# A hybrid decoder block on one core: the convolution's copies go to another queue, and one gate pair leaves the seven-product form

## The chip, the cores and the metric

The kernel runs on one core of one Trainium2 chip. The metric is device microseconds of one execution. Three runs of the kernel before gave 1552.89, 1555.58 and 1556.43 us; the median is 1555.58. One more execution was taken by the profiler, and every duration below is from it.

Five engines work in parallel, each through its own queue in order: TensorE (PE; its weight loads are listed as PEld), VectorE (DVE), ScalarE (ACT), GpSimd (POOL) and SyncE (SP, which here only starts DMAs). An instruction that waits holds up all that stands behind it on its engine. DMAs can be started from SP, ACT and POOL.

## What is computed

One decoder block over 256 tokens of width 2048, in fp32:

```python
proj = h_norm @ w_in          # q, k, v, g_out, gk_low, gate_b, gate_c, xc, merge_a, merge_b
o    = rmsnorm(gla_chunked(q, k, v, log_g), gla_norm_w)      # 4 heads, value width 512
y_a  = o * silu(g_out)
y_b  = gate_b * causal_depthwise_conv(gate_c * xc, conv_w)   # 3 taps: rows t, t-1, t-2
merged = sigmoid(merge_a) * y_a + sigmoid(merge_b) * y_b
h    = x + merged @ w_out
out  = rmsnorm(h + swiglu(rmsnorm(h, ffn_norm_w)), final_norm_w)
```

The change is in the stage that computes the six gate projections (g_out, gate_b, gate_c, xc, merge_a, merge_b, each 2048 columns), the convolution, and `merged`.

## The kernel before

**Pieces.** Every weight matrix is read in pieces of 128 x 1024 fp32 (512 KB), two blocks of 128 input rows by 512 columns. Each fp32 number is split into two rounded parts: ACT casts `hi` from `raw` (L217), DVE computes `lo = raw - hi` (L222). A product is then three matmuls (`mm3`, L326 to L328): lo with the high part of the activations, hi with their low part, hi with high. There are 5 `raw`, 6 `hi` and 5 `lo` buffers; `take` keeps 5 pieces loaded ahead of the one that PE uses. Each used piece is one tick of a counter.

**Eights.** A key such as `g0` (the first 512 columns of g_out; the digit is the group of 512 columns, 0 to 3) is 8 pieces of 12 matmuls, 6 for each half of the tokens. Its two sums lie in the PSUM banks `b5` and `ax1`, the same two for every key. After the last piece a function `done` reads them out. So a key's first 6 matmuls wait until `b5` has been read out, the next 6 until `ax1` has.

**Sevens.** A pair of keys (`gc0` with `xc0`, say) can be computed with seven block products in place of eight, `sevens` (L374), in four quarters: per quarter the plain block "11", the sums "t1", "t3", "t2", "t4", and later "21" and "22". That is 28 pieces of 6 matmuls, 168, where two keys as eights take 16 pieces of 12, 192. The price is on the other engines: 28 casts and 28 subtractions in place of 16, and one DVE sum for each of the 16 t-pieces (L238, L244), made in place in a tile `x` that ACT and DVE must first have read.

**The gate stage.** `GATES` (L73) lists six steps. A step names one pair for sevens and the keys for eights; `mixed` (L105) spreads the pieces of the eights over the gaps between the 28 pieces, first behind the t-pieces. In the kernel before the steps are: g0 alone; gc0+xc0 with ma0, gb0; gc1+xc1 with mb0, g1, ma1; gc2+xc2 with gb1, mb1, g2, ma2; gc3+xc3 with gb2, mb2; gb3+mb3 with g3, ma3. So five of twelve pairs are sevens.

What happens behind a key, for group i: `g` makes `ya` = silu(g) * o; `ma` multiplies `ya` by sigmoid(ma); `gb` is copied to `sb`; `mb` multiplies `sb` by sigmoid(mb) and then calls `merge`. The two sigmoids are done in `gated` (L843): ACT writes the sigmoid of one token half into a tile `scr` (L847), of which there is one buffer, and DVE multiplies (L848). The pair gc+xc gives `u` = gate_c * xc (L882).

**The convolution.** Two ticks later `conv_shift` (L805) has ACT start six DMAs (L814 to L819) that copy `u` into `u1` and `u2`, one and two tokens later; the taps come by one more (L811). Eight ticks later `conv_sum` (L821) has DVE make five operations on 128 x 1024, three products (L827 is u2's, L828 u1's, L829 u's) and two sums (L830, L831). `merge` (L833) multiplies `sb` by that, adds `ya` (L835, L836), and puts the four 128 x 128 transposes of each token half (L544) into PE's order, then ACT's and DVE's split of them (L546, L547) into `mh`, `ml`, which the output projection `wo` reads.

The ticks of `later` and `at` give the order in which the program issues the work. A scheduler behind it then orders each engine's queue by what it reckons to be ready, so the queues don't follow the ticks strictly. The sums of input blocks that sevens need are made from x at ticks 34, 40, 46, 52 (`x_blocks`, L710), in the attention stage, ahead of the gate stage.

After the gate stage, `wo` runs (4 keys as eights, other banks); the pool `ew` of the gate stage is closed behind wo0, and POOL loads x again into its place (L926) for the residual sum (L928). Then the feed-forward part, with five more pairs as sevens.

Of the kernel before, what the change touches and what calls it, by code (L numbers as in the profile page):

```python
# [43 lines left out]
def plan():  # L44
# [27 lines left out]

GATES = (  # L73
    (None, ("g0",)),
    (("gc0", "xc0"), ("ma0", "gb0")),
    (("gc1", "xc1"), ("mb0", "g1", "ma1")),
    (("gc2", "xc2"), ("gb1", "mb1", "g2", "ma2")),
    (("gc3", "xc3"), ("gb2", "mb2")),
    (("gb3", "mb3"), ("g3", "ma3")),
)  # L80

HIDDEN = (
# [16 lines left out]
def seven_list(pair):  # L99

    out = [(what, q) for q in range(4) for what in ("11", "t1", "t3", "t2", "t4")]
    return [(pair, e) for e in out + [(what, q) for q in range(4) for what in ("21", "22")]]


def mixed(step, early=False):  # L105

    pair, keys = step
    eights = [(key, k) for key in keys for k in range(0, KC, 2)]
    if pair is None:
        return eights  # L110
    sevens = seven_list(pair)
    sums = ("t1", "t3", "t2", "t4")
    gaps = [0] * len(sevens)
    rest = len(eights)
    while rest > 0:
        for some in (sums + ("11",) if early else sums, ("21", "22")):
            for n, (_, e) in enumerate(sevens):
                if e[0] in some and rest > 0:
                    gaps[n] += 1
                    rest -= 1  # L120
    out, put = [], 0
    for e, n in zip(sevens, gaps):
        out += [e] + eights[put:put + n]
        put += n
    return out


def gates_list():
    return [e for i, step in enumerate(GATES) for e in mixed(step, i == 4)]


def hidden_list(part):
# [33 lines left out]
def block_kernel(ctx, tc, x, xt, cols_in, gkw_in, gku_in, gnw, conv_w, finw, w_in, w_out, w_gu, w_dn, out):  # L166
# [7 lines left out]
    junk_pool = ctx.enter_context(tc.tile_pool(name="junk", bufs=1))  # L174
# [117 lines left out]
    def later(delay, fn):  # L292

        pending.append((count["tick"] + delay, fn))
# [15 lines left out]
    def one_at_a_time(delay, fn):  # L310

        spaced.append((count["tick"] + delay, fn))
# [189 lines left out]
                                op=ALU.subtract)  # L502

    xv = x.rearrange("(t p) d -> p t d", p=P)


    xs0 = wraw.tile([P, 4, T], F32, tag="raw", name="xs")
# [5 lines left out]


    def square_sum(src, acc):
        junk = junk_pool.tile([P, 512], mybir.dt.bfloat16, tag="junk", name="junk")
        nc.scalar.activation(junk[:, :src.shape[-1]], src, AF.Square, accum_out=acc)

    def rstd_of(ss, n, r):
# [20 lines left out]
    def transpose_block(src, t, hi, lo):  # L540

        ps = bank([P, 4, P], "trb", "ax0")
        for j in range(4):
            nc.tensor.transpose(out=ps[:, j, :], in_=src[:, j * P:(j + 1) * P], identity=ident)  # L544
# [148 lines left out]
    def at(tick, fn):  # L693
        later(tick - count["tick"], fn)
# [15 lines left out]
    def x_blocks(q):  # L710
        pair = gpool.tile([P, NM, T], F32, tag="bc", name="xraw")
        raw, work = pair[:, 0:4, :], pair[:, 4:8, :].rearrange("p s (j c) -> p s j c", c=P)
        cs = slice(4 * q, 4 * q + 4)
        nc.vector.tensor_tensor(out=raw, in0=xh[:, cs, :].bitcast(F32), in1=xl[:, cs, :].bitcast(F32), op=ALU.add)
        sum_blocks(raw, q, xsums, work)

    for q in range(4):
        at(34 + 6 * q, lambda q=q: x_blocks(q))


    def decayed(i, kr, qr):
# [78 lines left out]
    oside = None  # L800
    mix = ExitStack()
    mh, ml = [None] * 4, [None] * 4
    us, ya, sb = {}, {}, {}

    def conv_shift(i):  # L805
# [3 lines left out]
        us[i] = (us[i], u1, u2, taps)  # L809
        u = us[i][0]  # L810
        nc.scalar.dma_start(taps, conv_w[:, :, i * 512:(i + 1) * 512].to_broadcast([P, 3, 512]))  # L811
        nc.gpsimd.memset(u1[0:1, 0, :], 0.0)
        nc.gpsimd.memset(u2[0:2, 0, :], 0.0)
        nc.scalar.dma_start(u1[1:113, :, :], u[0:112, :, :])  # L814
        nc.scalar.dma_start(u1[113:128, :, :], u[112:127, :, :])
        nc.scalar.dma_start(u1[0:1, 1, :], u[127:128, 0, :])
        nc.scalar.dma_start(u2[2:114, :, :], u[0:112, :, :])
        nc.scalar.dma_start(u2[114:128, :, :], u[112:126, :, :])
        nc.scalar.dma_start(u2[0:2, 1, :], u[126:128, 0, :])  # L819

    def conv_sum(i):  # L821
        u, u1, u2, taps = us[i]

        def taps_of(j):
            return taps[:, j:j + 1, :].to_broadcast([P, NT, 512])

        nc.vector.tensor_tensor(out=u2, in0=u2, in1=taps_of(0), op=ALU.mult)  # L827
        nc.vector.tensor_tensor(out=u1, in0=u1, in1=taps_of(1), op=ALU.mult)  # L828
        nc.vector.tensor_tensor(out=u, in0=u, in1=taps_of(2), op=ALU.mult)  # L829
        nc.vector.tensor_tensor(out=u1, in0=u1, in1=u2, op=ALU.add)  # L830
        nc.vector.tensor_tensor(out=u, in0=u, in1=u1, op=ALU.add)  # L831

    def merge(i, ts):  # L833

        nc.vector.tensor_tensor(out=sb[i][:, ts, :], in0=sb[i][:, ts, :], in1=us[i][0][:, ts, :], op=ALU.mult)  # L835
        nc.vector.tensor_tensor(out=sb[i][:, ts, :], in0=sb[i][:, ts, :], in1=ya[i][:, ts, :], op=ALU.add)  # L836
        if mh[i] is None:
            mh[i] = omain.tile([P, 4, T], F32R, tag=f"m{i}", name="mh")
            ml[i] = oside.tile([P, 4, T], F32R, tag=f"m{i}", name="ml")
        for t in range(ts.start, ts.stop):  # L840
            one_at_a_time(2, lambda t=t: transpose_block(sb[i][:, t, :], t, mh[i], ml[i]))

    def gated(dst, ps):  # L843

        for t in range(NT):
            scr = ew.tile([P, 512], F32, tag="scr", name="scr")
            nc.scalar.activation(scr, ps[t], AF.Sigmoid, scale=r1[:, t:t + 1])  # L847
            nc.vector.tensor_tensor(out=dst[:, t, :], in0=dst[:, t, :], in1=scr, op=ALU.mult)  # L848

    def gate(key):  # L850
        i = int(key[-1])

        def done(ps):
            if key[:-1] == "g":
                ya[i] = ew.tile([P, NT, 512], F32, tag="ya", name="ya")
                for t in range(NT):
                    nc.scalar.activation(ya[i][:, t, :], ps[t], AF.Silu, scale=r1[:, t:t + 1])
                nc.vector.tensor_tensor(out=ya[i], in0=ya[i], in1=o[i], op=ALU.mult)
            elif key[:-1] == "gb":
                sb[i] = ew.tile([P, NT, 512], F32, tag="sb", name="sb")  # L860
                for t in range(NT):
                    nc.scalar.activation(sb[i][:, t, :], ps[t], AF.Copy, scale=r1[:, t:t + 1])
            elif key[:-1] == "ma":
                gated(ya[i], ps)
            else:
                gated(sb[i], ps)
                merge(i, slice(0, NT))

        return done

    def gate_pair(pair):
        i = int(pair[0][-1])

        def second(t):
            to = us if pair[0][:-1] == "gc" else sb
            if i not in to:
                to[i] = ew.tile([P, NT, 512], F32, tag="u" if to is us else "sb", name="u" if to is us else "sb")
            return to[i][:, t, :]

        def done(t, one, two):  # L880
            if pair[0][:-1] == "gc":
                nc.vector.scalar_tensor_tensor(out=two, in0=one, scalar=r1sq[:, t:t + 1], in1=two,  # L882
                                               op0=ALU.mult, op1=ALU.mult)
                if t == 0:
                    later(2, lambda: conv_shift(i))
                    later(8, lambda: conv_sum(i))
            else:
                nc.scalar.activation(two, two, AF.Sigmoid, scale=r1[:, t:t + 1])
                nc.vector.scalar_tensor_tensor(out=two, in0=one, scalar=r1[:, t:t + 1], in1=two,
                                               op0=ALU.mult, op1=ALU.mult)  # L890

                later(3 if t else 1, lambda: merge(i, slice(t, t + 1)))

        return second, done
# [22 lines left out]
    h = dpool = None  # L917
# [138 lines left out]
    assert not pending and not spaced and not ready and count["loaded"] == len(stream) + 1  # L1056


H_AT = (2, 4, 6, 8)
SQ_AT = (5, 7, 9, 11)  # L1060
WARM = 9
# [54 lines left out]
```

## Time and profile before

| what | us |
|---|---|
| median of 3 runs | 1555.58 |
| the profiled execution | 1552.18 |
| its span, first to last instruction | 1550.3 |
| PE busy in it | 1508.5 |
| DVE busy | 1205.4 |
| ACT busy | 839.4 |
| POOL busy | 20.8 |
| gate stage, first to last matmul of a gate | 212.5 to 744.8 |
| step 1 (gc0) begins | 236.3 |
| step 2 (gc1) | 319.1 |
| step 3 (gc2) | 431.0 |
| step 4 (gc3) | 560.6 |
| step 5 (gb3 with mb3) | 653.1 |

Times are from the start of the span. A row of the timeline gives start, duration, engine, line, operation, out<-in and, in brackets, the idle time of the engine just before and what ended it. A row of the waits reads "who waited for whom: us in total, times, longest". A row by windows gives, for a stretch, its length and the busy time and number of instructions of each engine, then the granted clock, the share of DMA time and GB/s. An engine name with a q is its sequencer, which issues DMAs and waits.

### The profile page before, as it was taken

To read this page: it belongs to the slowest core of one execution; us is meant where nothing else is said; L and a number is where in the kernel's file an instruction comes from. 1 tells how busy PE (TensorE), PEld (TensorE's weight loads), DVE (VectorE), ACT (ScalarE), POOL (GpSimd) and SP (SyncE) were. 2 spreads that over 40 slices of the span, in tenths; PEclk is the share of its full clock that TensorE was granted. 3 is DMA by queue.
4 is the path that set the end of the run, shared out by engine and by line. 5 is a ranking of instruction groups with operands and counts; after the bars stand their busy time and mean duration, and the time that the engine had idled before them with its cause. 6 is when DMAs were issued, how large, how long until landed. Compare 5 with 4: busy or idle time off the path is not lost.

```text
span 1550.3 us, 19386 instructions
## 1 busy us (share of the span) xinstructions
PE 1508.5 (97%) x7129; PEld 1256.5 (81%) x7129; DVE 1205.4 (78%) x1208; ACT 839.4 (54%) x947; POOL 20.8 (1%) x33
## 2 busy tenths in 40 slices
PE   9989999989999999889999999999999999999997
PEld 8979988868878787668788888788888888888887
DVE  5887548989879778989768998955889975678664
ACT  6755446645645545456556565633555553455543
POOL 0020000000000000000000000000000000000000
PEclk9999999999999999999999999999999999999999
DMA  9645557877876868768865777866676886676862
GB/s 318 219 149 164 174 162 251 275 237 240 277 229 215 296 176 269 233 209 284 308 181 162 245 229 254 301 206 188 203 262 206 272 281 192 182 222 200 249 222 90
DMA packets 98182, 350.18 MB, mean 226 GB/s; under 512 B 11084, under 2 KB 11212, under 8 KB 97960
## 3 DMA queue, kind: packets, MB, share of 16 engines
q1 hardware_dynamic: 94080, 337.97, 67.3%
q10 hardware_dynamic: 3432, 8.89, 2.3%
q0 software_dynamic: 576, 2.10, 0.4%
q8 instruction: 56, 0.92, 0.2%
q14 instruction: 38, 0.31, 0.1%
HBM read 342.64 MB, written 2.10 MB: 222 GB/s over the span
## 4 chain that ended last, share of the span: by engine, by line
PE 85%; DVE 5%; DMA 4%; issue 2%; ACT 2%; POOL 1%; ACTq 0%; SPq 0%; DVEq 0%
PE fg L326 7%; PE fg L328 7%; PE fg L327 7%; PE dn L326 5%; PE dn L328 5%; PE dn L327 5%; DVE lo L222 3%; PE fu L326 3%; PE fu L327 3%; PE fu L328 3%; PE gc L326 2%; PE gc L328 2%; PE gc L327 2%; DMA raw<-in_w_in_dram 2%; PE ma L326 2%
## 5 line engine op out<-in xcount | busy, mean ns | idle before, releaser
L222 DVE TENSOR_TENSOR lo<-raw,hi 128x1024 fp32r<-128x1024 f32 (+1 forms) x513 | 621.6, 1218 | 194.2 <-PE dn L326 76.3
L217 ACT CAST hi<-raw 128x1024 fp32r<-128x1024 f32 (+1 forms) x513 | 532.8, 1049 | 372.9 <-PE dn L328 116.0
L217 ACT CAST hi<-x 128x1024 fp32r<-128x1024 f32 x120 | 126.3, 1053 | 230.6 <-DVE x L244 153.4
L222 DVE TENSOR_TENSOR lo<-x,hi 128x1024 fp32r<-128x1024 f32 x120 | 146.8, 1223 | 45.4 <-ACT hi L217 32.3
L326 PE MATMUL dn<-lo,acth 128*128 128x512 f32 (+1 forms) x376 | 141.6, 377 | 0.3 <-ACT sg L965 0.3
L327 PE MATMUL dn<-hi,actl 128*128 128x512 f32 (+1 forms) x376 | 141.2, 376 | 0.0
L328 PE MATMUL dn<-hi,acth 128*128 128x512 f32 (+1 forms) x376 | 141.1, 376 | 0.0
L326 PE MATMUL fg<-lo,hh 128*128 128x512 f32 x312 | 122.6, 393 | 0.0
L327 PE MATMUL fg<-hi,hl 128*128 128x512 f32 x312 | 121.6, 390 | 0.0
L328 PE MATMUL fg<-hi,hh 128*128 128x512 f32 x312 | 121.5, 390 | 0.0
L244 DVE TENSOR_TENSOR x<-x,raw 128x1024 f32<-128x1024 f32 x80 | 97.6, 1220 | 4.9 <-DMA raw<-in_w_in_dram 2.6
L326 PEld LDWEIGHTS dn<-lo,acth 128*128 128x128 f32 x376 | 70.8, 188 | 13.4 <-ACT sg L965 0.7
L328 PEld LDWEIGHTS dn<-hi,acth 128*128 128x128 f32 x376 | 70.8, 188 | 12.8
L327 PEld LDWEIGHTS dn<-hi,actl 128*128 128x128 f32 x376 | 70.8, 188 | 12.6
L326 PE MATMUL fu<-lo,hh 128*128 128x512 f32 x192 | 74.7, 389 | 0.0
L328 PE MATMUL fu<-hi,hh 128*128 128x512 f32 x192 | 74.7, 389 | 0.0
L327 PE MATMUL fu<-hi,hl 128*128 128x512 f32 x192 | 74.7, 389 | 0.0
L328 PEld LDWEIGHTS fg<-hi,hh 128*128 128x128 f32 x312 | 58.6, 188 | 12.4
L326 PEld LDWEIGHTS fg<-lo,hh 128*128 128x128 f32 x312 | 58.6, 188 | 12.3 <-ACT hraw L534 0.3
L327 PEld LDWEIGHTS fg<-hi,hl 128*128 128x128 f32 x312 | 58.6, 188 | 11.7
L326 PE MATMUL fg<-lo,sh 128*128 128x512 f32 x160 | 62.9, 393 | 0.0
L328 PE MATMUL fg<-hi,sh 128*128 128x512 f32 x160 | 62.4, 390 | 0.0
(256 smaller groups left out, 3060.6 us busy)
## 6 DMA issues: line engine op xcount, KB each, us to landing
raw<-in_w_in_dram SPq DMA_DIRECT2D x255, 512.0 KB, 4.5
raw<-in_w_gu_dram SPq DMA_DIRECT2D x176, 512.0 KB, 4.5
raw<-in_w_dn_dram SPq DMA_DIRECT2D x88, 512.0 KB, 3.6
raw<-in_w_out_dram SPq DMA_DIRECT2D x32, 512.0 KB, 4.5
y<-in_w_in_dram SPq DMA_DIRECT2D x20, 512.0 KB, 5.3
x<-in_w_in_dram SPq DMA_DIRECT2D x20, 512.0 KB, 4.5
y<-in_w_gu_dram SPq DMA_DIRECT2D x20, 512.0 KB, 5.2
x<-in_w_gu_dram SPq DMA_DIRECT2D x20, 512.0 KB, 6.7
```

Source lines behind the costliest of these rows:

```text
L217: nc.scalar.copy(hi[:, ks, :], raw[:, ks, :])
L222: nc.vector.tensor_tensor(out=lo[:, ks, :], in0=raw[:, ks, :], in1=hi[:, ks, :].bitcast(F32), op=ALU.subtract)
L244: nc.vector.tensor_tensor(out=x, in0=x, in1=other, op=ALU.add)
L326: nc.tensor.matmul(ps, lhsT=sh, rhs=ml, start=first, stop=False, skip_group_check=onto)
L327: nc.tensor.matmul(ps, lhsT=sl, rhs=mh, start=False, stop=False, skip_group_check=onto)
L328: nc.tensor.matmul(ps, lhsT=sh, rhs=mh, start=False, stop=last, skip_group_check=onto)
```

## The change

Of the gate pairs, gb3 with mb3 is no longer sevens; four pairs are, and the steps are cut anew. `seven_list` puts the "21" and "22" pieces in another order, in the feed-forward part too. The convolution's taps and copies are started by POOL (`nc.gpsimd`), one tick after the product in place of two, and each of its five DVE operations has a tick of its own, 12 to 16 ticks after the copies' start. `merge` of group i waits at least until 19 ticks after the product, its sum is one tick behind its product, and its transposes three ticks. `gated` writes the sigmoid back into the PSUM bank, and DVE reads it there; the tile `scr` is gone. `ya` has two buffers in turn. `x_blocks` go from ticks 34, 40, 46, 52 to 42, 47, 52, 57. The scratch of `square_sum` lies in another pool.

```diff
@@ GATES
     (None, ("g0",)),
-    (("gc0", "xc0"), ("ma0", "gb0")),
-    (("gc1", "xc1"), ("mb0", "g1", "ma1")),
-    (("gc2", "xc2"), ("gb1", "mb1", "g2", "ma2")),
-    (("gc3", "xc3"), ("gb2", "mb2")),
-    (("gb3", "mb3"), ("g3", "ma3")),
+    (("gc0", "xc0"), ("ma0", "gb0", "mb0")),
+    (("gc1", "xc1"), ("g1", "ma1", "gb1")),
+    (("gc2", "xc2"), ("mb1", "g2", "ma2")),
+    (("gc3", "xc3"), ("gb2", "mb2", "g3", "ma3")),
+    (None, ("gb3", "mb3")),
@@ seven_list
-    return [(pair, e) for e in out + [(what, q) for q in range(4) for what in ("21", "22")]]
+    twos = (("21", 0), ("21", 1), ("22", 0), ("21", 2), ("22", 1), ("21", 3), ("22", 2), ("22", 3))
+    return [(pair, e) for e in out + list(twos)]
@@ gates_list
-    return [e for i, step in enumerate(GATES) for e in mixed(step, i == 4)]
+    return [e for step in GATES for e in mixed(step, step[1][0] == "gb2")]
@@ x_blocks
-        at(34 + 6 * q, lambda q=q: x_blocks(q))
+        at(42 + 5 * q, lambda q=q: x_blocks(q))
@@ conv_shift, conv_sum -> conv
-        nc.scalar.dma_start(taps, conv_w[:, :, i * 512:(i + 1) * 512].to_broadcast([P, 3, 512]))
+        nc.gpsimd.dma_start(taps, conv_w[:, :, i * 512:(i + 1) * 512].to_broadcast([P, 3, 512]))
         nc.gpsimd.memset(u1[0:1, 0, :], 0.0)
         nc.gpsimd.memset(u2[0:2, 0, :], 0.0)
-        nc.scalar.dma_start(u1[1:113, :, :], u[0:112, :, :])
-        nc.scalar.dma_start(u1[113:128, :, :], u[112:127, :, :])
-        nc.scalar.dma_start(u1[0:1, 1, :], u[127:128, 0, :])
-        nc.scalar.dma_start(u2[2:114, :, :], u[0:112, :, :])
-        nc.scalar.dma_start(u2[114:128, :, :], u[112:126, :, :])
-        nc.scalar.dma_start(u2[0:2, 1, :], u[126:128, 0, :])
+        nc.gpsimd.dma_start(u1[1:113, :, :], u[0:112, :, :])
+        nc.gpsimd.dma_start(u2[2:114, :, :], u[0:112, :, :])
+        nc.gpsimd.dma_start(u1[113:128, :, :], u[112:127, :, :])
+        nc.gpsimd.dma_start(u2[114:128, :, :], u[112:126, :, :])
+        nc.gpsimd.dma_start(u1[0:1, 1, :], u[127:128, 0, :])
+        nc.gpsimd.dma_start(u2[0:2, 1, :], u[126:128, 0, :])
...
+        for n, (dst, src, by, op) in enumerate(((u1, u1, 1, ALU.mult), (u2, u2, 0, ALU.mult), (u, u, 2, ALU.mult),
+                                                (u1, u1, u2, ALU.add), (u, u, u1, ALU.add))):
+            by = taps_of(by) if isinstance(by, int) else by
+            later(CONV_AT + n, lambda d=dst, s=src, y=by, o=op: nc.vector.tensor_tensor(out=d, in0=s, in1=y, op=o))
@@ merge
-        nc.vector.tensor_tensor(out=sb[i][:, ts, :], in0=sb[i][:, ts, :], in1=us[i][0][:, ts, :], op=ALU.mult)
-        nc.vector.tensor_tensor(out=sb[i][:, ts, :], in0=sb[i][:, ts, :], in1=ya[i][:, ts, :], op=ALU.add)
+        nc.vector.tensor_tensor(out=v, in0=v, in1=us[i][:, ts, :], op=ALU.mult)
+        later(1, lambda: nc.vector.tensor_tensor(out=v, in0=v, in1=ya[i][:, ts, :], op=ALU.add))
...
-            one_at_a_time(2, lambda t=t: transpose_block(sb[i][:, t, :], t, mh[i], ml[i]))
+            one_at_a_time(3, lambda t=t: transpose_block(sb[i][:, t, :], t, mh[i], ml[i]))
@@ gated
-            scr = ew.tile([P, 512], F32, tag="scr", name="scr")
-            nc.scalar.activation(scr, ps[t], AF.Sigmoid, scale=r1[:, t:t + 1])
-            nc.vector.tensor_tensor(out=dst[:, t, :], in0=dst[:, t, :], in1=scr, op=ALU.mult)
+            nc.scalar.activation(ps[t], ps[t], AF.Sigmoid, scale=r1[:, t:t + 1])
+            nc.vector.tensor_tensor(out=dst[:, t, :], in0=dst[:, t, :], in1=ps[t], op=ALU.mult)
@@ gate
-                ya[i] = ew.tile([P, NT, 512], F32, tag="ya", name="ya")
+                ya[i] = ew.tile([P, NT, 512], F32, tag=f"ya{i % 2}", name="ya")
...
-                merge(i, slice(0, NT))
+                at(max(count["tick"] + 1, merge_at.get(i, 0)), lambda: merge(i, slice(0, NT)))
@@ gate_pair
-                    later(2, lambda: conv_shift(i))
-                    later(8, lambda: conv_sum(i))
+                    later(1, lambda: conv(i))
+                    merge_at[i] = count["tick"] + CONV_AT + 7
...
+CONV_AT = 12
```

More of the change, by code (lines that the diff above doesn't have):

```diff
@@ L173, in block_kernel @@
     wlo = ctx.enter_context(tc.tile_pool(name="wlo", bufs=5))
-    junk_pool = ctx.enter_context(tc.tile_pool(name="junk", bufs=1))
     aT = ctx.enter_context(tc.tile_pool(name="aT", bufs=1))
@@ L504, in block_kernel @@
     xv = x.rearrange("(t p) d -> p t d", p=P)
+    dpool = None
     xs0 = wraw.tile([P, 4, T], F32, tag="raw", name="xs")
@@ L515, in square_sum @@
     def square_sum(src, acc):
-        junk = junk_pool.tile([P, 512], mybir.dt.bfloat16, tag="junk", name="junk")
+        junk = (dpool or gpool).tile([P, 512], mybir.dt.bfloat16, tag="junk", name="junk")
         nc.scalar.activation(junk[:, :src.shape[-1]], src, AF.Square, accum_out=acc)
@@ L802, in block_kernel, with conv @@
     mh, ml = [None] * 4, [None] * 4
-    us, ya, sb = {}, {}, {}
-    def conv_shift(i):
+    us, ya, sb, merge_at = {}, {}, {}, {}
+    def conv(i):
+        u = us[i]
         u1 = ew.tile([P, NT, 512], F32, tag="u1", name="u1")
@@ L808, in conv_shift @@
         taps = ew.tile([P, 3, 512], F32, tag="taps", name="taps")
-        us[i] = (us[i], u1, u2, taps)
-        u = us[i][0]
-        nc.scalar.dma_start(taps, conv_w[:, :, i * 512:(i + 1) * 512].to_broadcast([P, 3, 512]))
+        nc.gpsimd.dma_start(taps, conv_w[:, :, i * 512:(i + 1) * 512].to_broadcast([P, 3, 512]))
         nc.gpsimd.memset(u1[0:1, 0, :], 0.0)
         nc.gpsimd.memset(u2[0:2, 0, :], 0.0)
-        nc.scalar.dma_start(u1[1:113, :, :], u[0:112, :, :])
-        nc.scalar.dma_start(u1[113:128, :, :], u[112:127, :, :])
@@ L824, in taps_of @@
+        nc.gpsimd.dma_start(u1[0:1, 1, :], u[127:128, 0, :])
+        nc.gpsimd.dma_start(u2[0:2, 1, :], u[126:128, 0, :])
         def taps_of(j):
             return taps[:, j:j + 1, :].to_broadcast([P, NT, 512])
[L827 to L830, printed above, removed]
@@ L831, in conv_sum @@
-        nc.vector.tensor_tensor(out=u, in0=u, in1=u1, op=ALU.add)
+        for n, (dst, src, by, op) in enumerate(((u1, u1, 1, ALU.mult), (u2, u2, 0, ALU.mult), (u, u, 2, ALU.mult),
+                                                (u1, u1, u2, ALU.add), (u, u, u1, ALU.add))):
+            by = taps_of(by) if isinstance(by, int) else by
+            later(CONV_AT + n, lambda d=dst, s=src, y=by, o=op: nc.vector.tensor_tensor(out=d, in0=s, in1=y, op=o))
     def merge(i, ts):
-        nc.vector.tensor_tensor(out=sb[i][:, ts, :], in0=sb[i][:, ts, :], in1=us[i][0][:, ts, :], op=ALU.mult)
@@ L836, in merge @@
-        nc.vector.tensor_tensor(out=sb[i][:, ts, :], in0=sb[i][:, ts, :], in1=ya[i][:, ts, :], op=ALU.add)
+        v = sb[i][:, ts, :]
+        nc.vector.tensor_tensor(out=v, in0=v, in1=us[i][:, ts, :], op=ALU.mult)
+        later(1, lambda: nc.vector.tensor_tensor(out=v, in0=v, in1=ya[i][:, ts, :], op=ALU.add))
         if mh[i] is None:
@@ L916, in block_kernel @@
     ssh = const.tile([P, NT, 4], F32, name="ssh")
-    h = dpool = None
+    h = None
     for n in range(4):
```

2 lines of the change are left out of this document (removed).

## The prediction

> **What bounds the kernel now.** The first part of the page says which engine is full, and the windows then say where it is not.
>
> ```profile
> span 1550.3 us, 19386 instructions
> PE 1508.5 (97%) x7129; PEld 1256.5 (81%) x7129; DVE 1205.4 (78%) x1208; ACT 839.4 (54%) x947; POOL 20.8 (1%) x33
> ```
>
> PE is idle for 1550.3 - 1508.5 = 41.8 us. Windows by step of the gate stage (steps 1 to 5):
>
> ```profile
> core 0: us, PE busy (x) PEld busy (x) DVE busy (x) ACT busy (x) POOL busy (x), PEclk, DMA share, GB/s
> 236.30:319.10 82.80, 82.17 (x362) 67.44 (x361) 77.30 (x71) 53.29 (x55) 0.00 (x0) 1.00 0.78 258
> 319.10:431.00 111.90, 106.25 (x465) 87.47 (x464) 96.91 (x91) 59.29 (x63) 1.03 (x2) 0.97 0.78 250
> 431.00:560.60 129.60, 126.93 (x562) 104.22 (x561) 106.09 (x98) 69.86 (x74) 1.03 (x2) 1.00 0.75 241
> 560.60:653.10 92.50, 85.19 (x370) 67.62 (x368) 79.47 (x75) 45.92 (x51) 1.03 (x2) 1.00 0.72 228
> 653.10:745.00 91.90, 84.15 (x364) 67.40 (x364) 82.13 (x78) 51.08 (x54) 0.00 (x0) 1.00 0.76 246
> ```
>
> A pipelined matmul looks busy for 0.39 us, but the next starts sooner. The timeline around the longest stall of the stage gives the pace and the anatomy:
>
> ```profile
> 321.80 0.39 PE L326 MATMUL mb<-lo,xh 128*128 128x512 f32 x1
> 322.20 0.63 ACTq L814 DMA_DIRECT2D u<-u  x1
> 326.37 1.30 ACTq L819 DMA_DIRECT2D u<-u  x1
> 327.77 1.05 ACT L217 CAST hi<-raw 128x1024 fp32r<-128x1024 f32 x1 [5.10 <-DVE raw L238]
> 329.74 0.39 PE L328 MATMUL gc<-hi,sh 128*128 128x512 f32 x1
> 330.63 1.23 DVE L828 TENSOR_TENSOR u<-u,taps 128x1024 f32<-128x1024 f32 x1 [3.77 <-DMA u<-u]
> 334.50 1.22 DVE L222 TENSOR_TENSOR lo<-raw,hi 128x1024 fp32r<-128x1024 f32 x1
> 335.64 1.22 DVE L222 TENSOR_TENSOR lo<-x,hi 128x1024 fp32r<-128x1024 f32 x1
> 335.77 0.79 PE L326 MATMUL mb<-lo,xh 128*128 128x512 f32 x1 [5.65 <-DVE lo L222]
> 336.37 0.63 PE L327 MATMUL mb<-hi,xl 128*128 128x512 f32 x1
> ```
>
> From 321.80 to 329.74 PE starts 36 matmuls (two keys' pieces of 12, two sevens pieces of 6) without a gap, so one costs 7.94 / 35 = 0.2268 us. DVE's subtractions follow each other in 335.64 - 334.50 = 1.14 us. The reader is to see two blockades in it. ACT starts the six copies from 322.20 to 327.67 and casts nothing in that time; DVE then stands for 3.77 us in front of the first convolution product until a copy lands; PE runs out of `lo` and waits 5.65 us, and the first matmuls after it take 0.63 in place of 0.39 us (the only step where the granted clock is below 1.00, 0.97).
>
> A group of four transposes takes 0.44 us, and seven of the eight lie in these steps:
>
> ```profile
> 370.40 0.44 PE trb L544 x4
> ```
>
> With 360, 456, 552, 360 and 360 matmuls in steps 1 to 5, PE needs 81.6, 103.4, 125.2, 81.6 and 81.6 us, and 3.1 for the transposes: 476.7 of the 508.7 us. So **32 us are lost in steps 1 to 5**; step by step (transposes counted) 1.2, 7.6, 3.5, 10.0 and 9.9. The waits in this window name the cause; PE's longest in total, and DVE's two longest:
>
> ```profile
> PE gb L326 <- DVE lo L222: 7.5, 7, 2.1
> ```
>
> ```profile
> DVE lo L222 <- ACT hi L217: 34.1, 35, 2.7
> DVE u L828 <- DMA u<-u: 15.3, 4, 5.0
> ```
>
> DVE, late with `lo`, is the bound there. In steps 4 and 5 its own work (79.5 and 82.1 us) is 96% and 100% of what PE needs, with waits for ACT and for the copies on top. Step 1 has no convolution and loses only 1.2 us at 77.3 / 81.6 = 95%.
>
> **The change part by part.** *One pair fewer in sevens.* It adds 192 - 168 = 24 matmuls: 24 x 0.2268 = **+5.4 us** on PE, with no cover. On DVE it takes away 12 subtractions and 16 sums, 28 x 1.14 = 31.9 us, and five half-tile operations net (seven that put the products together, less two gate products); their nearest row is the gate product:
>
> ```profile
> L848 DVE TENSOR_TENSOR ya<-ya,scr 128x512 f32<-128x512 f32 x8 | 5.5, 684 | 0.0
> ```
>
> So 3.4 us more, 35.3 in all: DVE's 441.9 us in the five steps become about 407, while PE's 476.7 become 482.
>
> *The steps cut anew.* Moving keys as eights (8 subtractions, 9.1 us of DVE, against 96 matmuls, 21.8 us of PE) evens the shares out. Counted from the windows: step 1 gains mb0, 77.3 + 9.1 + 1.4 = 88 us of DVE against PE's 103.4 (85%); step 2 has gb1 for mb0, 95.5 against 104.3 (92%); step 3 loses gb1, 97 against 104.3 (93%); step 4 gains g3 and ma3, 79.5 + 20.8 = 100 against 126 (80%); step 5, plain, has 16 x 1.14 + 5 x 1.14 + 1.4 = 25 against 43.5 (58%). No step is above step 1 of before.
>
> *The copies on POOL.* ACT loses the issue time (5.5 us in the timeline above). What POOL pays is seen only at x's reload, beside ACT's copies of 448 KB:
>
> ```profile
> L926 POOL DMA_DIRECT2D h<-in_x_dram x4: 724/727/857, 758.5 to 760.8; - x4
> DMA to landing us min/median/max: 6.7/8.1/10.9
> u<-u ACTq DMA_DIRECT2D x8, 448.0 KB, 6.6
> ```
>
> Six copies and the taps at 0.73 us are 5.1 us of an engine that is 1% busy; from issue to landing 8.1 in place of 6.6. `u1` is then whole about 3.6 + 8.1 = 12 us after `u`, `u2` about 13. Twelve ticks of a three-key step are 12 x 103.4 / 52 = 24 us, so in program order the sums would find them there. But queues don't follow program order: L827 stands ahead of L828 in the program, and
>
> ```profile
> L827 DVE TENSOR_TENSOR u<-u,taps x4: 1214/1216/1217, 340.2 to 671.3; 128x1024 f32<-128x1024 f32 x4
> ```
>
> first runs at 340.2, 9.6 us after it. I read L828's early place as a gap that ACT's issue block left in DVE's work (no casts, so no subtractions ready); without the block, older work fills it. I take DVE's wait as gone; the bounds are 0 and the old 15.3 us. Behind a waiting sum stand the subtractions, and PE behind them. On POOL, the copies pass only their own memsets; x's reload stands behind the last group's copies, which are through long before. SP issues nothing new.
>
> The Trainium skill, "SBUF — State Buffer", section "Who interferes with whom", speaks against such a move: a DMA started by GpSimd needs that engine to write descriptors, and a VectorE copy in a two-port mode locks it out. The same section exempts tensor_tensor, which shares only the read side; the gate stage's DVE rows are all tensor_tensor or scalar_tensor_tensor, so by that page the term is nothing, and if they did lock, it would be the slower rival below.
>
> *The sigmoid in PSUM.* Before, ACT's second sigmoid had to wait for the one `scr`:
>
> ```profile
> 273.05 0.69 ACT L847 ACTIVATE scr<-ma,r 128x512 f32<-128x512 f32 x1
> 275.34 0.68 DVE L848 TENSOR_TENSOR ya<-ya,scr 128x512 f32<-128x512 f32 x1
> 276.05 0.69 ACT L847 ACTIVATE scr<-ma,r 128x512 f32<-128x512 f32 x1 [0.61 <-DVE ya L848]
> 274.64 0.39 PE L326 MATMUL gb<-lo,xh 128*128 128x512 f32 x1
> 276.79 0.50 PE L326 MATMUL gb<-lo,xh 128*128 128x512 f32 x1 [0.63 <-ACT scr L847]
> ```
>
> Now it doesn't, but `b5` is free only after DVE's product (276.0 here), not after ACT (273.7). PE wanted it at 274.6: 1.4 us of stall at the first half's matmuls, in place of the 0.63 us of idle time ahead of the second half's at 276.8. Six such seams follow in the new order (ma0, mb0, ma1, mb1, ma2, mb2 before a key of eights), at 0 to 1.4 us, and one, ma3 into gb3, with no sevens piece between, at about 1.3: I take 6 x 0.5 + 1.3 = **4.3 us**. DVE reads PSUM at the same price (L928, h<-wo,h, below, 0.69). ACT writing PSUM has no row; 16 operations by at most 0.1 us either way, off the path.
>
> *What stays late.* Steps 1 to 4 without copies waiting: 1.2 us each, from step 1 of before, **4.8 us**; step 5 nothing.
>
> *`ya` twice, the merge in parts, the transposes.* Nothing on the path; PE's place for the last group moves to behind the fourth and sixth piece of wo0, and x's reload behind it, from about 12 us after wo0 begins to 17 (six pieces of 12 matmuls are 16.3, and the transposes). Its first quarter then lands at 17 + 0.7 + 6.7 = 24.4, where the residual sum wants it at 22.6:
>
> ```profile
> 767.65 0.69 DVE L928 TENSOR_TENSOR h<-wo,h 128x512 f32<-128x512 f32 x1 [0.53 <-PE wo L328]
> ```
>
> DVE has slack in wo, so 0; bounds -1.4 (a stall at the old transposes) and +2.
>
> *`x_blocks` eight ticks later.* PE loses 4.2 us at head 0's scores, and their DVE operation (L741) stands behind a block's:
>
> ```profile
> PE o_ps L326 <- ACT sch L744: 2.9, 1, 2.9
> PE o_ps L326 <- ACT scr L742: 1.3, 1, 1.3
> 98.19 1.22 DVE L714 TENSOR_TENSOR xraw<-xh,xl 128x1024 f32<-128x1024 f32 x1
> 104.13 1.23 DVE L440 TENSOR_TENSOR sl<-xraw,sh 128x1024 fp32r<-128x1024 f32 x1
> 105.28 0.43 DVE L741 COPY_PREDICATED scr<-mask,sc_ps 128x256 f32<-128x256 int8 x1
> ```
>
> But L714 ran as soon as its buffer was free, ahead of its tick; a later tick may change nothing. I take 0; bounds 0 and -6 (4.2 and the slow matmuls after the stall).
>
> The order of "21" and "22" moves loads of the same size past each other: 0, also in the feed-forward part, which PE fills.
>
> **Sum.** +5.4 - 32.0 + 4.3 + 4.8 = -17.5 us: 1552.2 becomes 1534.7 for the profiled execution. That lies 3.4 below the median 1555.58 of the runs, so the forecast is 1555.6 - 17.5 = **1538 us**.
>
> **The rivals.** *The sums still stand in front of the copies*, because the queue's order puts them early again: the change doesn't do what its ticks say. For: L828's place. Against: ACT no longer blocks. Step 3 of before, at 84% with a 5.0 us wait, lost 2.3 more than step 1; three such steps give +7 to +8: 1546. *POOL is starved by DVE* and the copies come late; this one ends slower. Two POOL operations of one size:
>
> ```profile
> 77.42 6.07 POOL L685 TENSOR_TENSOR exk<-bc 128x512 f32<-128x512 f32 x1 [26.88 <-DVE bc L669]
> 84.45 1.06 POOL L686 TENSOR_TENSOR exk<-exk,bc 128x512 f32<-128x512 f32 x1
> ```
>
> The first ran while DVE was full, the second while it wasn't: 5 us each, 35 for seven issues, and the copies land 43 us after `u`, 19 late. DVE then has 114, 116 and 119 us in steps 2 to 4 (PE 104, 104, 126): about 10 + 12 + 5, and 8 where the last merge holds up wo: 1573. It turns the sign once the sums wait some 9 us each, copies 33 us after `u`. Against: x's four issues took 0.72 to 0.86 us, one of them beside a subtraction. *The PSUM banks are held by DVE's backlog*: at 92% DVE is up to four subtractions (4.6 us) behind when the product is queued, and six seams cost 2.5 more each: 1553. *The blocks of x do move*: -6, 1532.
>
> **How the numbers follow.** Forecast 0.45, sums still waiting 0.20, banks held 0.13, blocks of x 0.12, starved POOL 0.10. This kernel's measurement tells about 0.2% (3.1 us) from no change: faster means below 1552.5, slower above 1558.7. Faster: 0.45 + 0.20 + 0.12 and half of the banks' case, 0.83; slower the starved POOL, 0.10; the same 0.07. The range runs from 1527 (the blocks' gain, and most of the late 4.8 gone) to 1555 (past the banks' case), and leaves out the starved POOL and the edges.
>
> **What would show it.** Right: no wait of DVE for u<-u; ACT without DMAs in the stage; PE's loss in steps 1 to 5 near 9 us, with waits of PE for DVE's gate products of at most 1.4 us each; step 5 in 45 us. Wrong: POOL's issues above 1 us; a DVE wait of several us at a convolution product; PE waiting for `lo` in steps 2 and 3 as long as before.

## The result, and the profile after

The changed kernel takes **1533.96 us** (median; 1530.48 to 1535.26), the kernel before, beside it, 1554.53 (1552.89 to 1556.43). The ratio is 0.9864, 95% interval 0.9842 to 0.9886: 20.6 us faster. The forecast was 1538, 17.5 us faster, in a range from 1527 to 1555. The profiled execution took 1535.26 us against 1552.18, 16.9 less.

First the page of the changed kernel, then its windows by step (the columns are those of the prediction's windows):

```profile
span 1533.6 us, 19370 instructions
PE 1510.4 (98%) x7153; PEld 1262.0 (82%) x7153; DVE 1173.5 (77%) x1173; ACT 832.1 (54%) x936; POOL 36.6 (2%) x61
```

```profile
237.10:342.40 105.30, 104.06 (x458) 85.47 (x458) 90.93 (x81) 62.61 (x64) 0.00 (x0) 1.00 0.77 251
342.40:448.70 106.30, 105.24 (x466) 86.05 (x465) 95.87 (x90) 60.52 (x63) 5.02 (x9) 1.00 0.77 255
448.70:557.90 109.20, 105.73 (x465) 85.80 (x464) 93.95 (x87) 59.79 (x63) 4.97 (x9) 1.00 0.77 248
557.90:685.80 127.90, 126.38 (x562) 104.07 (x561) 107.11 (x100) 72.97 (x76) 6.56 (x12) 1.00 0.82 255
685.80:729.50 43.70, 43.70 (x193) 36.19 (x194) 24.75 (x22) 18.11 (x19) 1.54 (x4) 1.00 0.73 212
```

PE needs 103.4, 104.3, 104.3, 126.1 and 43.5 us for the matmuls and transposes of these steps (0.2268 us a matmul, as before). So it loses 1.9, 2.0, 4.9, 1.8 and 0.2 us, **10.8 in all, where it lost 32**. The five steps last 492.4 us in place of 508.7, and those 16.3 us are nearly the whole difference of the spans, 16.7. The granted clock is 1.00 throughout.

What PE waits for from step 1 into wo, all rows, and DVE's wait for the copies:

```profile
PE gb L326 <- DVE ya L844: 3.0, 3, 1.5
PE g L326 <- DVE sb L844: 1.4, 1, 1.4
PE tr L532 <- DVE h L925: 1.4, 1, 1.4
PE ma L326 <- ACT ya L853: 1.0, 1, 1.0
PE gc L326 <- ACT ya L853: 0.8, 1, 0.8
PE trb L545 <- DVE sb L833: 0.5, 1, 0.5
PE gc L326 <- DVE lo L222: 0.5, 2, 0.3
```

```profile
DVE u L827 <- DMA u<-u: 7.8, 2, 4.4
```

In the gate stage of the kernel before, PE waited for `lo` 7.5, 5.6, 3.4 and 2.4 us (ahead of gb, mb, g and gc); now it is 0.5 us. In their place stand the waits that the change itself made: for DVE's gate product (L844 now), which must have left the PSUM bank, and for x's reload behind the later transposes. DVE still stands in front of the copies, half as long.

### The profile page after: what moved, and what is told of

Same layout as the page of the kernel before. It is cut to its first block, busy times and chain, and to the rows that moved or that the text cites. A ratio compares the mean times of both kernels' runs of the same rounds, so it can differ in the third digit from the quotient of the medians.

```text
span 1533.6 us, 19370 instructions
## 1 busy us (share of the span) xinstructions
PE 1510.4 (98%) x7153; PEld 1262.0 (82%) x7153; DVE 1173.5 (77%) x1173; ACT 832.1 (54%) x936; POOL 36.6 (2%) x61
## 4 chain that ended last, share of the span: by engine, by line
PE 92%; DVE 3%; issue 1%; ACT 1%; DMA 1%; POOL 1%; SPq 0%; DVEq 0%; ACTq 0%
PE fg L326 7%; PE fg L328 7%; PE fg L327 7%; PE dn L326 5%; PE dn L327 5%; PE dn L328 5%; PE gc L326 3%; PE fu L326 3%; PE fu L328 3%; PE fu L327 3%; PE gc L328 3%; PE gc L327 3%; PE gb L326 2%; PE wo L326 2%; PE mb L326 2%; PE gb L327 2%
## 5 line engine op out<-in xcount | busy, mean ns | idle before, releaser
L222 DVE TENSOR_TENSOR lo<-raw,hi 128x1024 fp32r<-128x1024 f32 (+1 forms) x517 | 628.1, 1219 | 231.3 <-PE dn L326 74.8
L217 ACT CAST hi<-raw 128x1024 fp32r<-128x1024 f32 (+1 forms) x517 | 539.9, 1050 | 409.1 <-PE dn L328 114.1
L217 ACT CAST hi<-x 128x1024 fp32r<-128x1024 f32 x108 | 113.7, 1053 | 185.6 <-DVE x L244 130.0
L222 DVE TENSOR_TENSOR lo<-x,hi 128x1024 fp32r<-128x1024 f32 x108 | 132.1, 1223 | 31.8 <-ACT hi L217 18.7
L244 DVE TENSOR_TENSOR x<-x,raw 128x1024 f32<-128x1024 f32 x72 | 87.9, 1220 | 7.2 <-DMA raw<-in_w_in_dram 3.5
```

Source lines behind the costliest of these rows:

```text
L217: nc.scalar.copy(hi[:, ks, :], raw[:, ks, :])
L222: nc.vector.tensor_tensor(out=lo[:, ks, :], in0=raw[:, ks, :], in1=hi[:, ks, :].bitcast(F32), op=ALU.subtract)
L244: nc.vector.tensor_tensor(out=x, in0=x, in1=other, op=ALU.add)
```

## The experiments

Times are medians; each ratio is to the kernel before, run beside it.

**e1: the gate steps of before, all else changed.** Of the changed kernel:

```diff
-    (("gc0", "xc0"), ("ma0", "gb0", "mb0")),
-    (("gc1", "xc1"), ("g1", "ma1", "gb1")),
-    (("gc2", "xc2"), ("mb1", "g2", "ma2")),
-    (("gc3", "xc3"), ("gb2", "mb2", "g3", "ma3")),
-    (None, ("gb3", "mb3")),
+    (("gc0", "xc0"), ("ma0", "gb0")),
+    (("gc1", "xc1"), ("mb0", "g1", "ma1")),
+    (("gc2", "xc2"), ("gb1", "mb1", "g2", "ma2")),
+    (("gc3", "xc3"), ("gb2", "mb2")),
+    (("gb3", "mb3"), ("g3", "ma3")),
```

> The changed kernel with one part undone: the gate steps of before, so gb3 with mb3 is again a pair in sevens; the copies on POOL, the spread sums and the sigmoid in PSUM stay. Theory (both parts are needed: the new groups relieve steps 4 and 5, the copies steps 2 to 4): PE has 5.4 us less to do, but steps 4 and 5 keep DVE at 96% and 100% of PE and lose about 14 us there; about 1543 us, 9 above the changed kernel, with DVE late with lo in steps 4 and 5. Rival 1 (the copies were the whole gain): 1534 - 5.4 = 1528 us. Rival 2 (the groups were the whole gain): 1554 us, as before.

Measured: 1535.03 us, ratio 0.9862 (0.9839 to 0.9884), as the changed kernel. The theory missed by 8 us; neither rival's number fits either. Its windows of steps 4 and 5:

```profile
553.80:641.40 87.60, 83.81 (x370) 67.94 (x368) 79.72 (x75) 47.17 (x51) 4.96 (x9) 1.00 0.79 243
641.40:729.50 88.10, 84.47 (x365) 67.48 (x366) 82.00 (x78) 50.34 (x54) 3.10 (x6) 1.00 0.78 254
```

DVE does the same work as before (79.7 and 82.0 us), PE needs the same 82.5 and 82.0, and yet PE loses 5.1 and 6.1 us, not 10.0 and 9.9. All five steps together lose 16.2 us here and 10.8 in the changed kernel: the new grouping saves 5.4 us of loss and adds 5.4 us of matmuls. **Its net is nothing.**

**e2: ACT starts the copies, and the sums stand at one tick.** With the new grouping kept:

```diff
-        nc.gpsimd.dma_start(u1[1:113, :, :], u[0:112, :, :])
+        nc.scalar.dma_start(u1[1:113, :, :], u[0:112, :, :])
...
-            later(CONV_AT + n, lambda d=dst, s=src, y=by, o=op: nc.vector.tensor_tensor(out=d, in0=s, in1=y, op=o))
+            later(7, lambda d=dst, s=src, y=by, o=op: nc.vector.tensor_tensor(out=d, in0=s, in1=y, op=o))
```

(the same for the taps and the other five copies)

> The changed kernel with the other part undone: the taps and the six copies are started by ACT again, and the five sums stand at one tick, eight behind the product; the new gate steps, the sigmoid in PSUM and the rest stay. Theory (both parts are needed): ACT is blocked for 5.5 us and DVE for about 4 us in each of four convolutions; steps 2 and 3 at 92% and 93% of PE lose 4 to 6 more each, steps 4 and 5 have slack and lose 1 to 2; 1543 us, between 1540 and 1548. Rival 1 (the copies were the whole gain): 1554 us or above, since PE has 5.4 us more than before. Rival 2 (the groups were the whole gain): 1534 us.

Measured: 1547.79 us, ratio 0.9945 (0.9925 to 0.9964), 13.8 above the changed kernel. It lies in the theory's range, but by e5 and e6 its two parts don't add up as thought.

**e3: the sigmoid in SBUF.** ACT writes it into the dead tile `o` of the group:

```diff
-            nc.scalar.activation(ps[t], ps[t], AF.Sigmoid, scale=r1[:, t:t + 1])
-            nc.vector.tensor_tensor(out=dst[:, t, :], in0=dst[:, t, :], in1=ps[t], op=ALU.mult)
+            nc.scalar.activation(scr[:, t, :], ps[t], AF.Sigmoid, scale=r1[:, t:t + 1])
+            nc.vector.tensor_tensor(out=dst[:, t, :], in0=dst[:, t, :], in1=scr[:, t, :], op=ALU.mult)
```

> The changed kernel, but ACT writes the gates' sigmoid into the tile o of its group, which is dead by then and lies in SBUF, one half per token half; so a bank is free after ACT, not after DVE. Theory (PE's waits for DVE's gate product at the seams are real stalls): the 3.0 us of gb and 1.4 us of g go, and the bank of ma3 into gb3 is free about 1.1 us sooner; 3 to 5 us faster, 1530 us. Rival (the seams only let DVE catch up, and its lateness shows at the next piece): 1534 us, with the waits moved to DVE lo.

Measured: 1531.35 us, ratio 0.9843 (0.9821 to 0.9865), 1.3 to 2.6 below the two measurements of the changed kernel (1532.63 in e8, 1533.96). Two of PE's waits in the same stretch:

```profile
PE trb L545 <- DVE sb L833: 2.2, 1, 2.2
PE gb L326 <- ACT o L843: 1.4, 2, 0.9
```

The 4.4 us for DVE's gate product are gone, but 1.4 us for ACT and 1.7 more at a transpose have come. The time lies between theory and rival. Part of the stall comes back at the next places; how much of it is a real price is not shown, as the lower bound of the gain, 1.3 us, is also the distance between the two measurements of the changed kernel.

**e4: the sums of the first three convolutions at 24 ticks.**

```diff
-            later(CONV_AT + n, lambda d=dst, s=src, y=by, o=op: nc.vector.tensor_tensor(out=d, in0=s, in1=y, op=o))
+            later(CONV_AT * (2 if i < 3 else 1) + n, lambda d=dst, s=src, y=by, o=op: nc.vector.tensor_tensor(out=d, in0=s, in1=y, op=o))
...
-                    merge_at[i] = count["tick"] + CONV_AT + 7
+                    merge_at[i] = count["tick"] + CONV_AT * (2 if i < 3 else 1) + 7
```

> The changed kernel with the sums of the first three convolutions 24 in place of 12 ticks behind the copies, and their merges 12 ticks later. Theory (the queue's order follows readiness, not ticks): DVE's first product stays 12 to 14 us behind the copies, and the third convolution still waits about 4.4 us for its copies; time unchanged within 1.5 us. Rival (the ticks hold): the first product comes 36 us or more behind the copies, the 4.4 us wait is gone, 1 to 3 us faster.

Measured: 1531.8 us, ratio 0.9845 (0.9823 to 0.9867). In its trace the first product runs at 356.3 us with the copies begun at 342.9, 13.4 behind; in the changed kernel it is 357.0 and 343.5, the same distance. The row gives the number, the shortest, median and longest in ns, and the first and last start; below it stand DVE's idle time in us and how often:

```profile
L827 DVE TENSOR_TENSOR u<-u,taps x12: 1217/1219/1227, 356.3 to 695.6; 128x1024 f32<-128x1024 f32 x12
  DMA u<-u: 6.2, 2
```

The wait for the copies stays (6.2 us in two). For this first product, 12 more ticks have moved nothing. The time, 0.8 below e8, says no more.

**e5: only the burst.** The line of e2's second hunk alone; the copies stay on POOL.

> The changed kernel with the five sums of a convolution issued at one tick, seven behind the copies, as a burst; the copies stay on POOL. It splits the 13.8 us by which the run with ACT's copies and the burst is slower. Theory (the block of ACT by the copies' issue is what costs; the ticks of the sums don't bind the queue): within 2 us of the changed kernel, 1532 to 1536. Rival (the early burst costs, as DVE stands in front of the copies): about 10 us slower, 1544.

Measured: 1531.44 us, ratio 0.9848 (0.9833 to 0.9863). As theory: no gain from the spread of the sums is to be seen. Its tick does move the first product a little, to 10.0 us behind the copies (352.7 against 342.7), and DVE's wait for them is 9.1 us in three places; the kernel is not slower for it.

```profile
L827 DVE TENSOR_TENSOR u<-u,taps x12: 1218/1220/1226, 352.7 to 697.1; 128x1024 f32<-128x1024 f32 x12
  DMA u<-u: 9.1, 3
```

**e6: only the queue.** The first hunk of e2 alone (taps and six copies on ACT), the sums spread.

> The changed kernel with only the queue of the taps and the six copies undone: ACT starts them; the sums keep a tick each, 12 to 16 behind. Theory (ACT's block costs): three stalls of PE of 4 to 5 us, each with slow matmuls behind it, at the begin of steps 2 to 4; 10 to 14 us slower than the changed kernel, 1544 to 1548. Rival (the burst costs): within 3 us of it.

Measured: 1553.6 us, ratio 0.9996 (0.9983 to 1.0008): **the whole gain is gone** with the queue of seven DMAs, 21 us, more than the 10 to 14 of the theory. The stall at the begin of step 3, rows of ACT, DVE, SP and PE in order of time:

```profile
455.89 0.59 ACTq L814 DMA_DIRECT2D u<-u  x1
...
459.25 1.22 DVE L238 TENSOR_TENSOR raw<-y,x 128x1024 f32<-128x1024 f32 x1
459.36 0.52 SPq L211 DMA_DIRECT2D raw<-in_w_in_dram  x1
462.44 1.05 ACT L217 CAST hi<-raw 128x1024 fp32r<-128x1024 f32 x1 [5.68 <-PE gc L328]
...
468.02 1.23 DVE L244 TENSOR_TENSOR x<-x,raw 128x1024 f32<-128x1024 f32 x1 [7.56 <-DMA raw<-in_w_in_dram]
469.17 1.22 DVE L827 TENSOR_TENSOR u<-u,taps 128x1024 f32<-128x1024 f32 x1
469.28 0.33 SPq L274 DMA_DIRECT2D raw<-in_w_in_dram  x1
470.30 1.22 DVE L222 TENSOR_TENSOR lo<-raw,hi 128x1024 fp32r<-128x1024 f32 x1
471.58 0.80 PE L326 MATMUL mb<-lo,xh 128*128 128x512 f32 x1 [5.61 <-DVE lo L222]
472.17 0.63 PE L327 MATMUL mb<-hi,xl 128*128 128x512 f32 x1
```

ACT issues the six copies from 455.89 to 462.31 and casts nothing until 462.44. But that is not the wait that ends last. At 463.5 it has cast the next piece, and PE still has matmuls until 466. DVE could subtract, and doesn't: the next instruction in its queue is a sum (L244) that needs the weight load started at 459.36, and behind that stands the convolution's product (L827), and only then the subtractions. In the chain that ended last, this load, which ran beside the copies, stands in front of L244, and no work of ACT:

```profile
459.36 8.58 DMA raw<-in_w_in_dram
```

DVE so waits 7.56 us, meanwhile frees no `raw` buffer, so that SP starts no load from 459.36 to 469.28; PE waits 5.61 us for `lo`, and the matmuls behind take 0.63 us. At the begin of step 2 it is again such a load (DVE waits 5.41 us, PE 3.39). At the begin of step 4 DVE stands 10.01 us in front of the product, for the copies themselves, PE 4.48; there ACT's run of issues is in the chain, since it starts the fifth copy only 5.4 us after the first.

The changed kernel has the same instructions on DVE, and in another order. Behind L238 three subtractions come ahead of L244:

```profile
454.00 1.22 DVE L238 TENSOR_TENSOR raw<-y,x 128x1024 f32<-128x1024 f32 x1
455.28 1.22 DVE L222 TENSOR_TENSOR lo<-x,hi 128x1024 fp32r<-128x1024 f32 x1
456.42 1.22 DVE L222 TENSOR_TENSOR lo<-raw,hi 128x1024 fp32r<-128x1024 f32 x1
458.01 1.23 DVE L222 TENSOR_TENSOR lo<-y,hi 128x1024 fp32r<-128x1024 f32 x1 [0.36 <-PE mb L326]
461.32 1.23 DVE L244 TENSOR_TENSOR x<-x,raw 128x1024 f32<-128x1024 f32 x1 [2.08 <-DMA raw<-in_w_in_dram]
```

The edit doesn't touch DVE's program: the scheduler orders that queue. That it puts the subtractions back because it reckons with ACT's issues is likely, but not shown. So the choice of queue is shown to cost the 21 us; how much of them is ACT's time and how much the order of DVE's queue, no run separates.

In the changed kernel POOL issues the six copies in 3.2 us and nobody waits for POOL:

```profile
343.54 0.61 POOL L814 DMA_DIRECT2D u<-u  x1 [119.09 <-DVE u L879]
...
346.20 0.52 POOL L819 DMA_DIRECT2D u<-u  x1
```

That e6 is 5.8 us slower than e2, which has the burst on top, was not expected and stays open. One difference in the traces is a wait of PE for ACT's silu, 2.9 us, that e6 has and e2 hasn't.

**e7: the input blocks on other buffers.**

```diff
-        pair = gpool.tile([P, NM, T], F32, tag="bc", name="xraw")
-        raw, work = pair[:, 0:4, :], pair[:, 4:8, :].rearrange("p s (j c) -> p s j c", c=P)
+        raw = gpool.tile([P, 4, T], F32, tag="vl", name="xraw")
+        work = gpool.tile([P, 4, 2, P], F32, tag="vh", name="xwork")
...
-        at(42 + 5 * q, lambda q=q: x_blocks(q))
+        at(34 + 3 * q, lambda q=q: x_blocks(q))
```

> The changed kernel with x_blocks made to run later by their buffers: their two tiles take the buffers of vh and vl, free only behind the second head's attention (about 121 us), in place of that of bc (free at 87 us); ticks 34, 37, 40, 43. Theory (their place in DVE's queue is set by the buffer, not by the tick, and it holds up head 0's scores): the waits of o_ps for ACT (2.9 and 1.8 us) fall below 1 us together, and the slow matmuls behind go too; 4 to 7 us faster, 1528. Rival (the scores are late for another reason, the tables before them): within 1.5 us.

Measured: 1526.15 us, ratio 0.9816 (0.98 to 0.9831), 6.5 below e8. In the changed kernel the blocks stand where they stood before, for all that their ticks are eight later:

```profile
98.31 1.22 DVE L715 TENSOR_TENSOR xraw<-xh,xl 128x1024 f32<-128x1024 f32 x1
105.40 0.43 DVE L742 COPY_PREDICATED scr<-mask,sc_ps 128x256 f32<-128x256 int8 x1
```

With the other buffers, L715 runs from 114.5 us on, the scores' operation at 101.13, and of 4.7 us of waits before head 0's products (2.9 and 1.8) there is one left, of 1.0:

```profile
101.13 0.45 DVE L742 COPY_PREDICATED scr<-mask,sc_ps 128x256 f32<-128x256 int8 x1
```

```profile
PE o_ps L326 <- ACT scr L743: 1.0, 1, 1.0
```

The granted clock from 107 to 113 us is 1.00 here; in the changed kernel, behind its waits, it is 0.66.

**e8: the changed kernel again.**

> The changed kernel itself, as it is, beside the others on one chip: 1534 us within 2, and how far it moves from call to call says which of the small differences count.

Measured: 1532.63 us, ratio 0.9856 (0.9839 to 0.9873), 1.3 from the first median. Differences of about that size are not counted here.

**e9: the kernel before, with POOL for ACT in the seven DMAs of `conv_shift`.**

```diff
-        nc.scalar.dma_start(u1[1:113, :, :], u[0:112, :, :])
+        nc.gpsimd.dma_start(u1[1:113, :, :], u[0:112, :, :])
```

> The kernel before with one thing changed: the taps and the six copies of each convolution are started by POOL in place of ACT. Theory (ACT's block is the whole cost of before that the change takes away): 1536 us within 3, as the changed kernel, with five pairs and all else as before. Rival (the gain needs the new grouping, the spread or the second ya buffer as well): 1543 us or above.

Measured: 1539.24 us, ratio 0.9907 (0.9886 to 0.9928). One word in seven lines brings 15.5 of the 20 us; it lies between theory and rival. By its windows PE loses 0, 4.9, 2.3, 4.6 and 8.5 us in the five steps, 20.3:

```profile
235.90:317.50 81.60, 81.60 (x362) 67.59 (x361) 76.09 (x70) 53.22 (x55) 0.00 (x0) 1.00 0.80 260
317.50:426.70 109.20, 106.34 (x465) 87.35 (x464) 96.98 (x91) 59.44 (x63) 5.00 (x9) 0.98 0.81 256
426.70:555.10 128.40, 126.64 (x562) 104.30 (x561) 106.47 (x99) 70.85 (x74) 4.95 (x9) 1.00 0.74 244
555.10:642.20 87.10, 83.87 (x369) 67.93 (x367) 79.58 (x75) 47.02 (x51) 5.00 (x9) 1.00 0.78 243
642.20:732.70 90.50, 85.48 (x364) 68.53 (x364) 81.63 (x77) 50.46 (x55) 3.14 (x6) 0.98 0.78 250
```

The ticks are those of before, and yet DVE waits 3.7 us for the copies in place of 15.3. In the first convolution seven subtractions now stand ahead of the first product, where two did, and this product waits 1.70 us:

```profile
DVE u L828 <- DMA u<-u: 2.0, 1, 2.0
DVE u L827 <- DMA u<-u: 1.7, 1, 1.7
```

From here to e1 (1535.03), with the same groups, are the second `ya`, the spread, the sigmoid, the later merges, the order of the copies and of the "21" and "22", the ticks of the blocks and the rest of the change together: 4.2 us. They were not taken apart, save that no gain is seen from the spread (e5) and the blocks' ticks move nothing (e7).

**e10 and e11: the best that the runs point to.** Both things that helped, e3's and e7's edits, on the changed kernel (e10) and on the gate steps of before (e11).

> The changed kernel with both things that helped: the blocks of x on later buffers and the sigmoid in the tile o. If the two add up (6.5 and 2 us): 1524 us. Rival (the time freed at one place is lost at the next): 1526 us, as with the blocks alone.

> The same as e10 with the gate steps of before, five pairs in sevens. The grouping alone changed nothing (1535 against 1534 us), so: 1525 us within 2. If the banks' waits weigh less with five pairs, 1522; if DVE is short of time in steps 4 and 5, 1528.

Measured: 1525.09 us, ratio 0.9812 (0.9792 to 0.9832), and 1528.64, ratio 0.9841 (0.9818 to 0.9865). e10 is the lowest median of all, 29.6 us below the kernel before beside it, but only 1.1 below e7, which is less than the changed kernel moved from one measurement to the next: that e3's edit adds to e7's is not shown. With five pairs it is 3.5 us slower, the third of the numbers expected; PE waits for `lo` there in three rows (3.3, 1.9 and 1.2 us), of which e10 has none.

**e12: two of the six copies on ACT.** In the changed kernel, the copies of 448 KB (L814, L815) back to `nc.scalar`, the rest on POOL.

> The changed kernel with the two large copies of each convolution (448 KB each) started by ACT and the taps and the four small ones by POOL. Theory (it is the time in which ACT issues, about 0.6 us a copy, more when its queue is full, that costs): ACT is blocked for 1.2 us in place of 6, and the time is within 3 us of the changed kernel, 1532 to 1536. Rival (copies from ACT's queue as such hold up the weight loads): 1545 us or above.

Measured: 1533.69 us, ratio 0.9867 (0.9846 to 0.9888): nothing lost. A large copy costs ACT 0.53 to 0.61 us, and its queue as such holds up nothing. At step 3 DVE's order, too, is that of the changed kernel: six subtractions stand between `u` and the sum that waits for a load (L244), two in e6. At step 2 it isn't: the product comes behind three subtractions and waits 2.18 us for its copy, and PE is not held up. What costs is a run of six, 6.4 us in e6, with the order that comes with it. Whether the number or the kind counts (the 14- and 15-row copies took ACT up to 2.34 us there), no run separates, and none shows a full queue.

## Why the prediction was right, and the step that was wrong

*The sum.* PE's price of 24 more matmuls and the loss that would remain were right: step 5 lasts 43.7 us against 43.5 forecast, and the loss left is 10.8 against 9.1. That the total came out is in part luck, since its two main parts did not do what they were credited with.

*The step that failed is the cause of the old loss in steps 4 and 5*, "DVE, late with lo, is the bound there. In steps 4 and 5 its own work ... is 96% and 100% of what PE needs", and with it the part "The steps cut anew", which was to free them. The prediction named "waits for ACT and for the copies on top", but looked for the cure in DVE's load. e1 has the same DVE work and loses 11.2 us there, not 19.9. The new groups (e1 to the changed kernel) bring as much as the matmuls cost. The copies' queue alone takes PE's loss in the five steps from 32 to about 20 us (e9), and putting it back in the changed kernel costs the whole gain again, 21 us (e6). A busy share said that DVE was full; it didn't say what DVE stood in front of. The first timeline did. ACT's 5.10 us without a cast end at 327.77, but DVE waits for a copy until 330.63 and, one row later, for a weight load:

```profile
333.36 1.23 DVE L244 TENSOR_TENSOR x<-x,raw 128x1024 f32<-128x1024 f32 x1 [1.50 <-DMA raw<-in_w_in_dram]
```

Only behind that come the subtractions, five in a row, that PE is waiting for. The prediction put ACT's issues down as 5.5 us that ACT loses, with no price on PE. It did see the mechanism in one sentence, "without the block, older work fills it", and gave it no share of the gain; e9 shows this refilling of DVE's queue with nothing changed but the copies' queue.

*The sums in front of the copies.* "I take DVE's wait as gone" was wrong by half: 7.8 of 15.3 us stay, none of it in steps 2 and 3. "Twelve ticks ... are 24 us" was wrong too: the first product of the first convolution comes 10.0, 13.5 and 13.4 us behind the copies at 7, 12 and 24 ticks (e5, the changed kernel, e4). The rival built on this wait gave 7 to 8 us of cost; steps 4 and 5, where both waits fall, lose 2.0 us in all. DVE has 107 us of work there to PE's 126 (100 were forecast), and 25 to 43.5.

*The seams.* 4.3 us were forecast; the waits for the gate product are 3.0 + 1.4 = 4.4. Right in size, but a price of 4.3 us of time is not shown: taking the waits away (e3) gains 1.3 to 2.6.

*x's reload.* Taken as 0 with a bound of +2: PE waits 1.4 us for the first residual sum.

*The blocks of x.* 0 was taken and 0 came, for the reason given, the buffer; e7 shows it by moving the buffer.

*POOL starved by DVE*, the slower rival: not so. POOL issued each six copies at 0.51 to 0.61 us apiece, in three of the four convolutions with DVE busy all the while. By the exemption of tensor_tensor in the Trainium skill, "SBUF — State Buffer", section "Who interferes with whom", nothing was to be expected, and the trace agrees.

## What to carry to other kernels

Before an engine that feeds the bottleneck is made to start DMAs in a run, don't go by its busy share. Read the longest stretch in which it does not do its feeding work; then read, on the engine behind it, which instruction waits for a transfer and how much ready work stands behind that in the queue, and what is freed late by it (buffers, then loads). Moving a DMA can also change the order of a queue that it doesn't stand in (e6, e9). "DMA: Bandwidth & Descriptors" in the Trainium skill, section "Issuing engines are not separate DMA queues", says that another engine only saves the issue time, which is "usually small relative to the DMA itself". For two large copies the trace agrees (e12); for all six the choice was worth 15.5 us (e9) to 21 us (e6) of 1554, with DVE's order changed along with the issue time. And where a scheduler orders the queues, check in the trace that a tick has moved an instruction before pricing the move; a buffer moved the blocks of x here (e7), their ticks didn't.

## What the runs showed of the hardware

The convolution's copies slow the weight loads beside them, whoever starts them: the three loads into `raw`, 512 KB each, that the changed kernel issues between 449.5 and 454.5 us, among its second convolution's copies, land after 8.2 to 9.2 us, the two issued from 440 to 448 after 4.3 to 4.4; in e6 the one issued at 456.96 takes 9.4. In the changed kernel DVE has subtractions to do meanwhile (e6 shows both).

```profile
DMA to landing us min/median/max: 8.2/8.4/9.2
```

```profile
DMA to landing us min/median/max: 4.3/4.4/4.4
```

A copy of 448 KB lands in 7.4 us (median) from POOL, 6.6 from ACT before.

Waits of PE of about 5.6 us leave slow matmuls behind them (0.63 in place of 0.39 us, in before and e6), and so do shorter ones: in e9 waits of 2.86 and 2.21 us are followed by matmuls of 0.63 us, the second at once:

```profile
655.92 0.80 PE L326 MATMUL gb<-lo,sh 128*128 128x512 f32 x1 [2.21 <-DVE lo L222]
656.51 0.63 PE L327 MATMUL gb<-hi,sl 128*128 128x512 f32 x1
```

The changed kernel's gate stage, where no wait is above 1.5 us, shows a granted clock of 1.00 in all five steps. The Trainium skill, "TensorE: Matmul & The Clock Gate", section "What's actually happening", puts the limit at an idle window of about 3.4 us; by e9's rows waits shorter than that were enough here.
